# A decoder block's FFN: up-projection with stationary activations, down-projection by a scheme of seven block products

## The chip, the core and the metric

One of the cores of a Trainium2 chip runs the kernel. The metric is the time of one execution on the device in microseconds (us). The profile is of one execution, and its times are microseconds from the first instruction.

TensorE (PE in the profile) multiplies a stationary operand that was loaded into it (PEld) with a moving one and adds into banks of PSUM. VectorE (DVE), ScalarE (ACT) and GpSimd (POOL) work on elements, SyncE (SP) issues transfers.

## What is computed

One layer with 256 tokens of 2048 channels. `mix` comes from a gated convolution, a causal pooling and a cross-attention into 256 memory tokens; the change leaves that part as it was. D_FF is 5632.

```python
h = rmsnorm(x, g_mix)
...
x = x + mix @ w_out
h = rmsnorm(x, g_ffn)
u = causal_dwconv(h @ w_up, ffn_conv_w) + ffn_conv_b     # 3 taps, per channel
gate, val = jnp.split(u, 2, axis=-1)                     # 5632 channels each
x = x + (silu(gate) * val) @ w_down
return rmsnorm(x, g_final)
```

## The kernel before

**Split precision.** Every factor of a product is held as two parts: a high part, rounded to the type that TensorE multiplies at full rate, and a low part, the rest. A product is three matmuls: high by high, low by high, high by low.

**The stream of weights.** All weights pass in tiles of 1 MB. `next_tile` hands out the next one and runs ahead: `load` issues the transfer on SyncE's queue three tiles ahead (three `raw` buffers), and two tiles ahead `split_piece` has ScalarE copy the high part (L129) and VectorE subtract it for the low part (L130), into three buffers each.

**Up-projection.** `unit_a` and its `mm_a` hold the weights stationary: for each chunk of 128 inputs and 128 outputs the weights' high part multiplies the activations' high and low parts side by side (512 columns, L306), their low part the high parts (256 columns, L309). The result lies with channels in the partitions and tokens in the columns. A unit is 256 channels of gate and of value; there are 22. `up_finish` adds the two halves and multiplies by the row of the tokens' norms (`gather`, L322 to L324), and applies the convolution: one ScalarE operation for the last tap and the bias (L747), two of VectorE for the other taps (L751), and silu for the gate (L755). `up` multiplies gate and value (L776) and splits them into the tile `u` (L777, L778).

**Down-projection.** The units are done in groups of 8, 7, 5 and 2. `down` holds the activations stationary and streams 512 columns of weights (`mm_b`, L338, L341, L344) into eight banks, and `add_in` adds these into the residual `xt` (L706). A group's down-projection stands after the next group's first unit. `down_last` does the last group, four chunks of 128 channels, in pieces with the final norm between them.

**Order.** In the first and the last part the instructions of an engine keep the order of the program. Elsewhere a scheduler sets each engine's order before the run, and from then on every engine works in that order.

Of the kernel before, what the change touches and what calls it, by code (L numbers as in the profile page):

```python
# [24 lines left out]
def kernel(  # L25
# [23 lines left out]
    psum = ctx.enter_context(tc.tile_pool(name="psum", bufs=8, space=bass.MemoryType.PSUM))  # L49

    def bank(name):
        return psum.tile([P, 512], F32, tag="bank", name=name)

# [17 lines left out]
    # Per-channel vectors, as columns of 128 channels, by transposing rows of 128.  # L71
# [20 lines left out]
    rows = lambda v: v.rearrange("(r c) -> r c", c=P)  # noqa: E731  # L92
# [10 lines left out]
    stream = []  # (source, nk, ncol, pieces)  # L103
# [4 lines left out]
    def load(i, between=None):  # L108
        src, nk, ncol, pieces = stream[i]
        raw = wpool.tile([P, nk, ncol], F32, tag="raw", name=f"raw_{i}")  # L110
# [23 lines left out]
    def split_tile(i):  # L134
        nk, pieces = stream[i][1], stream[i][3]
        step = nk // pieces
        for j in range(0, nk, step):
            split_piece(i, j, j + step)
        loaded.pop(i)
# [16 lines left out]
    n_units = NF // 2  # L156
    UNITS = [8, 7, n_units - 17, 2]  # sizes of FFN groups in units of 256 channels
# [20 lines left out]
    # The pool's weights: per pair of groups the three chunks' rows, in the columns of  # L178
    # the output chunks that they reach; wp_at[k] is the first of them.
# [17 lines left out]
    # Chunks of the mix in the order in which they come about.  # L197
# [10 lines left out]
    # A group's down-projection comes after the next group's first unit; that of the  # L208
    # last but one after all units.
    sched = []  # L210
    done = 0
    for gi, (a, n) in enumerate(group_of):
        upto = n_units if gi + 2 >= len(group_of) else a + n + 1
        for u in range(done, upto):
            sched.append(("up", u, [g for g, (b, m) in enumerate(group_of) if b <= u][-1]))
        done = upto
        sched.append(("down", gi, None))
    for what, a, b in sched:
        if what == "up" and a == 0:
            for h in (0, 1):  # L220
                plan_a(w_up, 0, (h,))
                plan_a(w_up, D_UP, (h,))
        elif what == "up":
            plan_a(w_up, a * 256)
            plan_a(w_up, D_UP + a * 256)
        else:
            a0, n = group_of[a]
            for n2 in range(2):
                plan_b(w_down, a0 * 2, n * 2, n2 * 1024, 1024, 2)

# [1 line left out]
    def turn_pair(xt, k, nm):  # L232
        pt = bank(f"pt_{nm}_{k}")
# [24 lines left out]
    def rstd_of(ssq, nm):  # L258
        """ssq [P, n] sums of squares -> 1 / sqrt(mean + eps), with a Newton step."""
# [14 lines left out]
    def row_of(r, nm):  # L274
        """[P, TB] per-token values -> the same row of S values in every partition."""
# [44 lines left out]
    def gather(ps, row, o, engine=nc.vector):  # L320
        """(main + corrections) * row -> o [P, S] in SBUF."""
# [4 lines left out]
    def mm_b(ps, wt, actT, ks, tbs, first, last):  # L326
        """ps[tb][n] += act[tokens of tb, chunk k] @ w[chunk k, columns of n]."""
# [398 lines left out]
    def up_matmul(u):  # L726
        if u:
            return [unit_a(h2T, f"g{u}"), unit_a(h2T, f"v{u}")]
# [197 lines left out]
```

## Time and profile before

| | |
|---|---|
| time, median of 3 runs | 1065.43 us (1064.88 to 1066.43) |
| span of the profiled execution, first to last instruction | 1064.7 us |
| TensorE busy | 1054.7 us, 99% |
| VectorE busy | 703.6 us, 66% |
| ScalarE busy | 529.0 us, 50% |
| GpSimd busy | 43.1 us, 4% |
| moved by DMA | 202.01 MB, mean 190 GB/s |

The profiled execution's own time is its span; no other time of it is given. A row of a group gives line, engine, operation, output and input with their shapes and the count, then the busy time and the mean of one in nanoseconds, then the engine's idle time ahead of them and what ended it. In a timeline a row is start, duration and instruction; rows that follow each other closely overlap. In the chain the share of an engine is the part of the span in which the end waited for it.

### The profile page before, as it was taken

The numbers are of one execution on the slowest core, as the hardware profiler recorded it, in microseconds if no ns is written. First come the engines' busy times: TensorE is split into PE (matmuls) and PEld (weight loads), VectorE is DVE, ScalarE is ACT, GpSimd is POOL, SyncE is SP. The second block draws the span as 40 slices with busy tenths as digits, with TensorE's granted clock in tenths as the row PEclk, the third lists the DMA queues.
The fourth block names the chain that finished last, engine by engine and source line by source line (L and its number), as shares of the span: only waits on it lengthen the run. The fifth ranks groups of instructions, "written<-read, shape, count | busy, mean of one in ns | idle before, by whom it ended". The sixth has DMA issues, their size and how long they took to land.

```text
span 1064.7 us, 14249 instructions
## 1 busy us (share of the span) xinstructions
PE 1054.7 (99%) x5632; PEld 907.2 (85%) x5632; DVE 703.6 (66%) x920; ACT 529.0 (50%) x683; POOL 43.1 (4%) x163
## 2 busy tenths in 40 slices
PE   9999999999999999999999999999999999999996
PEld 8888898888888888888888888888888888888885
DVE  5677786764556777777744467777754477777655
ACT  5965454443446655555533344554533345555343
POOL 0023500000000000000000000000000000000000
PEclk9999999999999999999999999999999999999998
DMA  9765465455555556555555555655555555654552
GB/s 316 243 224 172 143 206 189 161 195 183 186 185 174 184 196 198 188 181 185 198 198 198 196 171 187 198 185 175 195 198 197 191 174 190 198 177 178 198 198 80
DMA packets 147342, 202.01 MB, mean 190 GB/s; under 512 B 3619, under 2 KB 125771, under 8 KB 147147
## 3 DMA queue, kind: packets, MB, share of 16 engines
q1 hardware_dynamic: 147242, 201.09, 55.8%
q8 instruction: 44, 0.72, 0.3%
q14 instruction: 24, 0.19, 0.0%
q10 hardware_dynamic: 32, 0.01, 0.0%
HBM read 198.99 MB, written 2.10 MB: 189 GB/s over the span
## 4 chain that ended last, share of the span: by engine, by line
PE 98%; DVE 1%; ACT 0%; issue 0%; DVEq 0%
PE pa_v L306 15%; PE pa_g L306 15%; PE pa_g L309 7%; PE pa_v L309 7%; PE pd L338 7%; PE pd L344 7%; PE pd L341 7%; PE po L338 3%; PE po L341 3%; PE po L344 3%; PE pa_cc L306 2%; PE pa_cx L306 2%; PE pa_cb L306 2%; PE pa_pv L306 2%; PE pk L395 2%; PE pa_q L306 1%
## 5 line engine op out<-in xcount | busy, mean ns | idle before, releaser
L130 DVE TENSOR_TENSOR lo<-raw,hi 128x2048 fp32r<-128x2048 f32 (+2 forms) x196 | 425.5, 2172 | 271.6 <-ACT hi L129 270.6
L129 ACT ACTIVATE hi<-raw 128x2048 fp32r<-128x2048 f32 (+2 forms) x196 | 355.9, 1818 | 255.8 <-PE pd L344 98.4
L306 PE MATMUL pa_v<-h2T,hi 128*128 128x512 f32 x672 | 236.7, 396 | 0.0
L306 PE MATMUL pa_g<-h2T,hi 128*128 128x512 f32 x672 | 236.7, 396 | 0.0
L309 PE MATMUL pa_g<-h2T,lo 128*128 128x256 f32 x672 | 188.5, 281 | 0.0
L309 PE MATMUL pa_v<-h2T,lo 128*128 128x256 f32 x672 | 188.5, 281 | 0.0
L306 PEld LDWEIGHTS pa_v<-h2T,hi 128*128 128x128 f32 x672 | 126.0, 188 | 30.0
L306 PEld LDWEIGHTS pa_g<-h2T,hi 128*128 128x128 f32 x672 | 126.0, 188 | 30.0
L309 PEld LDWEIGHTS pa_g<-h2T,lo 128*128 128x128 f32 x672 | 127.0, 189 | 0.1
L309 PEld LDWEIGHTS pa_v<-h2T,lo 128*128 128x128 f32 x672 | 127.0, 189 | 0.0
L338 PE MATMUL pd<-hi,u 128*128 128x512 f32 x320 | 98.6, 389 | 0.0
L341 PE MATMUL pd<-lo,u 128*128 128x512 f32 x320 | 98.5, 389 | 0.0
L344 PE MATMUL pd<-hi,u 128*128 128x512 f32 x320 | 98.5, 389 | 0.0
L751 DVE SCALAR_TENSOR_TENSOR t<-h,cols,t 128x256 f32<-128x256 f32 x176 | 79.1, 480 | 2.2 <-ACT t L747 1.4
L755 ACT ACTIVATE t<-t 128x256 f32<-128x256 f32 x44 | 18.3, 418 | 107.0 <-DVE t L751 107.0
L341 PEld LDWEIGHTS pd<-lo,u 128*128 128x128 f32 x320 | 60.1, 188 | 12.6
L344 PEld LDWEIGHTS pd<-hi,u 128*128 128x128 f32 x320 | 60.1, 188 | 12.4
L338 PEld LDWEIGHTS pd<-hi,u 128*128 128x128 f32 x320 | 59.9, 188 | 12.4
L747 ACT ACTIVATE t<-h,cols 128x256 f32<-128x256 f32 x88 | 49.8, 593 | 0.0
L322 ACT ACTIVATE h<-pa_g 128x256 f32<-128x256 f32 x42 | 16.0, 380 | 61.3 <-PE pa_g L309 61.3
L338 PE MATMUL po<-hi,mixT 128*128 128x512 f32 x128 | 39.6, 391 | 0.0
L341 PE MATMUL po<-lo,mixT 128*128 128x512 f32 x128 | 39.5, 389 | 0.0
(207 smaller groups left out, 1280.9 us busy)
## 6 DMA issues: line engine op xcount, KB each, us to landing
raw<-in_w_up_dram SPq DMA_DIRECT2D x88, 1024.0 KB, 5.0
raw<-in_w_down_dram SPq DMA_DIRECT2D x44, 1024.0 KB, 4.9
raw<-in_w_in_dram SPq DMA_DIRECT2D x28, 1024.0 KB, 4.9
raw<-in_w_out_dram SPq DMA_DIRECT2D x16, 1024.0 KB, 4.9
raw<-in_w_kv_dram SPq DMA_DIRECT2D x4, 1024.0 KB, 5.2
raw<-in_w_kv_dram SPq DMA_DIRECT2D x6, 512.0 KB, 8.3
memt<-in_mem_dram SPq DMA_DIRECT2D x8, 256.0 KB, 7.7
xt<-in_x_dram SPq DMA_DIRECT2D x4, 512.0 KB, 6.7
```

The source lines that it names most:

```text
L129: nc.scalar.activation(hi[:, s, :], raw[:, s, :], AF.Copy)
L130: nc.vector.tensor_tensor(lo[:, s, :], raw[:, s, :], hi[:, s, :].bitcast(F32), op=ALU.subtract)
L306: nc.tensor.matmul(ps[mi], hi[:, kk, c], actT[:, k, :], start=first and kk == 0, stop=False)
L309: nc.tensor.matmul(ps[mi][:, S:], lo[:, kk, c], actT[:, k, :S], start=False, stop=last and kk == nk - 1,)
L322: nc.scalar.activation(o, ps[:, S:], AF.Copy)
L338: nc.tensor.matmul(ps[tb][n], ah, hi[:, kk, c], start=f, stop=False)
L341: nc.tensor.matmul(ps[tb][n], ah, lo[:, kk, c], start=False, stop=False)
L344: nc.tensor.matmul(ps[tb][n], al, hi[:, kk, c], start=False, stop=l)
L395: nc.tensor.matmul(psk[mi], wt[0][:, j, c], mT[:, k, :], start=k == 0, stop=False)
L747: nc.scalar.activation(t, hp[:, 2:], AF.Identity, bias=cvec("ffn_conv_b", m), scale=cw[2])
L751: nc.vector.scalar_tensor_tensor(t, hp[:, s : s + S], cw[s], t, op0=ALU.mult, op1=ALU.add)
L755: nc.scalar.activation(t, t, AF.Silu)
```

## The change

**Up-projection.** A unit is 512 channels; there are 11, in groups of two and a last one alone. `up(u, b)` does one weight tile, four chunks of inputs by 512 channels: for each of the two blocks of 128 tokens the activations are stationary and the weights move, 24 matmuls of 512 columns. The eight tiles of a unit are four of the gate and four of the value. The result has tokens in the partitions, so the norm becomes a scale per partition in ScalarE's copy out of PSUM (L842), and `up_finish` turns it back by eight transposes (L853) into PSUM, from which ScalarE (L861) and VectorE (L863) do the convolution. This is put off through `todo` until the first half of the next up tile is issued.

**Down-projection.** But for the last unit, the 8 chunks of a group and 1024 columns of output make a block (two blocks a group, ten in all). With the activations cut into four blocks (two token blocks by even and odd chunks) and the weights into four (b11, b12, b21, b22), seven products of 12 matmuls each stand for eight. `turn` makes the sums of activation blocks in `sums`, with their high and low parts (L895 to L905). The sums of weight blocks are made in three buffers of 1 MB as the stream runs: b11+b12 and then b22 by VectorE (L247), b12+b22 and b11+b21 by an accumulating transfer from buffer to buffer that GpSimd issues (`add_far`, L244). After its sum, each is split as a tile of the stream (L254, L255). The block b21 is loaded into the buffer of b12, and so after the fourth product's split. `prod` adds the bank of a chain into `xt` after each product (L933).

**Order of the stream.** The list `after` says how many products of the group before follow each up tile: in a group of 16 up tiles none after the first three, one after each of the next twelve, two after the last; in the last group of eight tiles one after each of six, then two, then six. The scheduler moves some of it.

**Buffers.** The PSUM banks are opened again for the FFN, five for up tiles and transposes and three for the products. `sums` and `ffn` take the place of the tiles `u`; the last unit's activations go into a part of `h2T`.

```diff
-    UNITS = [8, 7, n_units - 17, 2]  # sizes of FFN groups in units of 256 channels
+    n_units = NF // 4
+    UNITS = [2] * (n_units // 2) + [1]
...
+    class Blocks:
+        def __init__(self, seq, gi, p):
+            self.seq, self.gi, self.p = seq, gi, p
+            self.k0 = group_of[gi][0] * 4
+        def buf(self, name):
+            at = {"b11": 0, "b22": 1, "b12": 2, "b21": 2}[name]
+            return rawd[(self.seq + at) % 3]
+        def load(self, name):
+            s, h = int(name[1]) - 1, int(name[2]) - 1
+            c0 = self.p * 1024 + h * 512
+            src = w_down[self.k0 * P : (self.k0 + 8) * P, c0 : c0 + 512]
+            src = src.rearrange("(j s p) c -> s p j c", s=2, p=P)[s]
+            nc.sync.dma_start(self.buf(name), src)
+        def add_far(self, to, what):
+            nc.gpsimd.dma_start(self.buf(to), self.buf(what), accum_op=ALU.add)
+        def add(self, to, what):
+            nc.vector.tensor_tensor(self.buf(to), self.buf(to), self.buf(what), op=ALU.add)
+        def split(self, i, idx):
+            raw = self.buf(("b11", "b11", "b11", "b12", "b22", "b21", "b11")[idx])
+            hi, lo = split[i] = [
+                wpool.tile([P, 4, 512], F32R, tag=t, name=f"{t}_{i}") for t in ("hi", "lo")
+            ]
+            nc.scalar.activation(hi, raw, AF.Copy)
+            nc.vector.tensor_tensor(lo, raw, hi.bitcast(F32), op=ALU.subtract)
+            if idx == 0:
+                self.add("b11", "b12")
+                self.add_far("b12", "b22")
+            elif idx == 1:
+                self.add("b11", "b22")
+            elif idx == 3:
+                self.load("b21")
+                self.add_far("b11", "b21")
+            elif self.next is not None and idx >= 4:
+                self.next.load({4: "b11", 5: "b22", 6: "b12"}[idx])
...
-    sched = []
+    for gi, (a, n) in enumerate(group_of):
+        n_t = 8 * n
+        if not prods:
+            after = [0] * n_t
+        elif n == 2:
+            after = [0, 0, 0] + [1] * 12 + [2]
+        else:
+            after = [1, 1, 1, 1, 1, 1, 2, 6]
+        assert sum(after) == len(prods)
+        for t in range(n_t):
+            sched.append(("up", a + t // 8, t % 8))
+            for _ in range(after[t]):
+                sched.append(prods.pop(0))
+        if gi < len(group_of) - 1:
+            prods = [("prod", b, i) for b in blocks[2 * gi : 2 * gi + 2] for i in range(N_PROD)]
+    for what, a, b in sched:
+        if what == "up":
+            w, q = part_of(a, b)
+            plan_b(w_up, 4 * q, 4, w * D_UP + a * 512, 512, 4)
+        elif what == "prod":
+            stream.append((a, None, b, 1))
+    a0, n = group_of[-1]
+    for n2 in range(2):
+        plan_b(w_down, a0 * 4, n * 4, n2 * 1024, 1024, 2)
...
-    row_2 = None
-    u_tiles = {}
-    def up_matmul(u):
-        if u:
-            return [unit_a(h2T, f"g{u}"), unit_a(h2T, f"v{u}")]
-        ps = [[bank(f"pu0_{w}_{mi}") for mi in range(2)] for w in range(2)]
-        for h in range(2):
-            for w in range(2):
-                mm_a(ps[w], next_tile(), h2T, h * 8, 8, h == 0, h == 1)
-                if h == 0 and w == 0:
-                    transpose_in(xt, h2T, "g_ffn", range(8, 16), "x2")
-        return ps
...
+    psum_ctx.close()
+    for kind, n in (("pool", 5), ("prod", 3)):
+        psum[kind] = ctx.enter_context(
+            tc.tile_pool(name=f"psum_{kind}", bufs=n, space=bass.MemoryType.PSUM)
+        )
+    sums = apool.tile([P, N_PROD + 1, 2, 4, P], F32R, tag="act", name="sums")
+    ffn = apool.tile([P, 4, 2048], F32, tag="act", name="ffn")
+    u_raw = ffn[:, 0, :].rearrange("p (c t) -> p c t", t=S)
+    rawd = [ffn[:, 1 + i, :].rearrange("p (j c) -> p j c", c=512) for i in range(3)]
+    for name in ("b11", "b22", "b12"):
+        blocks[0].load(name)
+    u_last = h2T[:, : 4 * UNITS[-1], :]
+    up_ps, up_gates, todo, r_2 = {}, {}, [], []
+    def up(u, b):
+        w, q = part_of(u, b)
+        if q == 0:
+            up_ps[w] = [bank(f"pu{u}_{w}_{tb}") for tb in range(TB)]
+        ps = up_ps[w]
+        hi, lo = next_tile()
+        for tb in range(TB):
+            for kk in range(4):
+                k = 4 * q + kk
+                ah = h2T[:, k, tb * P : (tb + 1) * P]
+                al = h2T[:, k, S + tb * P : S + (tb + 1) * P]
+                for n, (x_, y_) in enumerate(((ah, hi), (ah, lo), (al, hi))):
+                    nc.tensor.matmul(
+                        ps[tb], x_, y_[:, kk, :],
+                        start=k == 0 and n == 0, stop=k == KC - 1 and n == 2,
+                    )
+            if tb == 0 and todo:
+                todo.pop(0)()
+            r_2.append(rstd_sum(ssq4, "x2"))
+        if q < 3:
+            return
+        z = []
+        for tb in range(TB):
+            z.append(spool.tile([P, 512], F32, tag="w2k", name=f"z_{u}_{w}_{tb}"))
+            nc.scalar.activation(z[tb], ps[tb], AF.Copy, scale=r_2[0][:, tb : tb + 1])
+        todo.append(lambda: up_finish(u, w, z))
+    def up_finish(u, w, z):
+        pt = []
+        for c in range(4):
+            if c % 2 == 0:
+                pt.append(bank(f"pz{u}_{w}_{c}"))
+            for tb in range(TB):
+                o = c % 2 * S + tb * P
+                nc.tensor.transpose(pt[-1][:, o : o + P], z[tb][:, c * P : (c + 1) * P], ident)
+        outs = []
+        for c in range(4):
+            v = pt[c // 2][:, c % 2 * S : (c % 2 + 1) * S]
+            m = w * NF + u * 4 + c
+            tag, n, bufs = ("w1k", S, 6) if w else ("hpad", PAD + S, HPAD)
+            t = spool.tile([P, n], F32, tag=tag, name=f"t_{u}_{w}_{c}", bufs=bufs)[:, :S]
+            cw = [cvec("ffn_conv_w", j * 2 * NF + m) for j in range(3)]
+            nc.scalar.activation(t, v, AF.Identity, bias=cvec("ffn_conv_b", m), scale=cw[2])
+            for s in (1, 2):
+                nc.vector.scalar_tensor_tensor(
+                    t[:, s:], v[:, : S - s], cw[2 - s], t[:, s:], op0=ALU.mult, op1=ALU.add
+                )
+            if w == 0:
+                nc.scalar.activation(t, t, AF.Silu)
+            outs.append(t)
+        if w == 0:
+            up_gates[u] = outs
+            return
+        gates = up_gates.pop(u)
+        gi = [g for g, (a, n) in enumerate(group_of) if a <= u][-1]
+        for c in range(4):
+            if gi < len(group_of) - 1:
+                o = u_raw[:, (u - group_of[gi][0]) * 4 + c, :]
+                nc.vector.tensor_tensor(o, gates[c], outs[c], op=ALU.mult)
+            else:
+                nc.vector.tensor_tensor(gates[c], gates[c], outs[c], op=ALU.mult)
+                split_into(u_last[:, c, :], gates[c])
+        if gi < len(group_of) - 1 and u == group_of[gi][0] + group_of[gi][1] - 1:
+            turn(gi)
+    def turn(gi):
+        v = u_raw.rearrange("p (j s) (b t) -> p s b j t", s=2, b=TB)
+        a11, a12, a21, a22 = v[:, 0, 0], v[:, 1, 0], v[:, 0, 1], v[:, 1, 1]
+        t = wpool.tile([P, 4, 4, P], F32, tag="raw", name=f"turn_{gi}")
+        tt = nc.vector.tensor_tensor
+        parts = [(0, a11), (5, a12), (6, a22)]
+        for at, src in parts:
+            nc.scalar.activation(sums[:, at, 0], src, AF.Copy)
+        tt(t[:, 0], a21, a22, op=ALU.subtract)
+        tt(t[:, 2], a11, a21, op=ALU.subtract)
+        tt(t[:, 1], t[:, 0], a11, op=ALU.subtract)
+        for at, src in parts[:1]:
+            tt(sums[:, at, 1], src, sums[:, at, 0].bitcast(F32), op=ALU.subtract)
+        tt(t[:, 3], t[:, 1], a12, op=ALU.add)
+        nc.scalar.activation(sums[:, 1:5, 0], t, AF.Copy)
+        for at, src in parts[1:]:
+            tt(sums[:, at, 1], src, sums[:, at, 0].bitcast(F32), op=ALU.subtract)
+        tt(sums[:, 1:5, 1], t, sums[:, 1:5, 0].bitcast(F32), op=ALU.subtract)
+    chains = {}
+    def prod(bl, i):
+        hi, lo = next_tile()
+        chain, first, tb, right, op = (
+            ("a", True, 0, 0, ALU.add),
+            ("b", True, 1, 1, ALU.add),
+            ("a", False, 0, 1, ALU.subtract),
+            ("a", False, 1, 1, ALU.subtract),
+            ("b", False, 0, 1, ALU.add),
+            ("c", True, 0, 0, ALU.add),
+            ("a", False, 1, 0, ALU.add),
+        )[i]
+        if first:
+            chains[chain] = bank(f"pp_{bl.seq}_{chain}", "prod")
+        ps = chains[chain]
+        for j in range(4):
+            ah, al = sums[:, i, 0, j, :], sums[:, i, 1, j, :]
+            for n, (a, b) in enumerate(((ah, hi), (ah, lo), (al, hi))):
+                nc.tensor.matmul(
+                    ps, a, b[:, j, :], start=first and j == 0 and n == 0,
+                    stop=j == 3 and n == 2, skip_group_check=True,
+                )
+        c0 = bl.p * 1024 + right * 512
+        o = xt[:, tb, c0 : c0 + 512]
+        nc.vector.tensor_tensor(o, o, ps, op=op)
+        while todo and bl.gi == len(blocks) // 2 - 1 and i == 2:
+            todo.pop(0)()
...
```

**Where the instructions stand.** The first place is the start of the last group, on VectorE. Before, a unit's end on VectorE looked like this (`lo` is a weight tile's low part, `t` and `h` the unit's channels, `u` the activations for the down-projection, `pa` PSUM):

```order
L776 TENSOR_TENSOR t_0_1_7106<-t_0_1_7106,t_1_1_7203 128x256
L130 TENSOR_TENSOR lo_7256<-raw_7215,hi_7255 128x2048
L778 TENSOR_TENSOR u_6376<-t_0_0_7096,u_6376 128x256
L778 TENSOR_TENSOR u_6376<-t_0_1_7106,u_6376 128x256
L323 TENSOR_TENSOR h_0_0_7291<-pa_g_0_7213,h_0_0_7291 128x256
L324 TENSOR_TENSOR h_0_0_7291<-h_0_0_7291,row_x_3031 128x256
L130 TENSOR_TENSOR lo_7316<-raw_7253,hi_7315 128x2048
```

Now, after the last unit of the last whole group, the sums of activations follow (`turn` is their scratch tile, `ffn` at L247 two weight blocks):

```order
L877 TENSOR_TENSOR ffn<-t_0_3_6861,t_1_3_7107 128x256
L900 TENSOR_TENSOR sums<-ffn,sums 128x512
L896 TENSOR_TENSOR turn_7115<-ffn 128x512
L904 TENSOR_TENSOR sums<-ffn,sums 128x512
L898 TENSOR_TENSOR turn_7115<-turn_7115,ffn 128x512
L904 TENSOR_TENSOR sums<-ffn,sums 128x512
L901 TENSOR_TENSOR turn_7115<-turn_7115,ffn 128x512
L247 TENSOR_TENSOR ffn<-ffn 128x2048
L905 TENSOR_TENSOR sums<-turn_7115,sums 128x4x512
L933 TENSOR_TENSOR xt<-xt,pp_a 128x512
L136 TENSOR_TENSOR lo_7162<-raw_7140,hi_7161 128x2048
```

The first product needs the low sum of L900, the next one that of L905; between them stand five smaller operations and one sum of weight blocks.

On TensorE the first product of that group stands behind the second up tile, one tile later than the list says (`hi_7069` is that tile's high part, `hi_7048` the first product's):

```order
L827 MATMUL pu_0_1_7068<-hi_7069,h2T 128x512
L927 MATMUL pp_a<-hi_7048,sums 128x512 [waits Activation_49]
L927 MATMUL pp_a<-lo_7049,sums 128x512
L927 MATMUL pp_a<-hi_7048,sums 128x512 [waits DVE_49]
L927 MATMUL pp_a<-hi_7048,sums 128x512
```

The third of these is the first that uses a low part of the activations' sums, and waits for VectorE, which makes it.

The second place is ScalarE at the seventh product of a block. Before, in a down-projection stretch, the high parts followed each other:

```order
L777 ACTIVATE u_7813<-t_0_1_8107 128x256
L129 ACTIVATE hi_8280<-raw_8248 128x2048
L129 ACTIVATE hi_8310<-raw_8278 128x2048
L129 ACTIVATE hi_8340<-raw_8308 128x2048
L129 ACTIVATE hi_8378<-raw_8338 128x2048
```

Now (with the semaphores waited for; DMASW is a transfer that GpSimd issued, `z` the copies of an up tile out of PSUM):

```order
L254 ACTIVATE hi_6975<-ffn 128x2048 [waits DMAHW7_49,DVE_49,PE_49]
L254 ACTIVATE hi_6995<-ffn 128x2048 [waits DMASW7_49,DVE_49,PE_49]
L842 ACTIVATE z_1_0_7024<-pu_1_0_6818,r_x_2908 128x512 [waits PE_49]
L842 ACTIVATE z_1_1_7026<-pu_1_1_6819,r_x_2908 128x512 [waits PE_49]
L135 ACTIVATE hi_7028<-raw_6993 128x2048 [waits DMAHW6_49,DVE_49]
```

Behind the high part that waits for the accumulating transfer (`hi_6995`) stand the copies of the up tile and the next tile's high part.

More of the change, by code (lines that the diff above doesn't have):

```diff
@@ L48, with bank @@
     spool = ctx.enter_context(tc.tile_pool(name="spool", bufs=2))
-    psum = ctx.enter_context(tc.tile_pool(name="psum", bufs=8, space=bass.MemoryType.PSUM))
-    def bank(name):
-        return psum.tile([P, 512], F32, tag="bank", name=name)
+    psum_ctx = ExitStack()
+    psum = {"pool": psum_ctx.enter_context(tc.tile_pool(name="psum", bufs=8, space=bass.MemoryType.PSUM))}
+    def bank(name, kind="bank"):
+        if "prod" not in psum:
+            return psum["pool"].tile([P, 512], F32, tag="bank", name=name)
+        return psum["prod" if kind == "prod" else "pool"].tile([P, 512], F32, tag=kind, name=name)
     ident = cpool.tile([P, P], F32, name="ident")
@@ L135, in split_tile @@
         nk, pieces = stream[i][1], stream[i][3]
+        if nk is None:
+            stream[i][0].split(i, stream[i][2])
+            return
         step = nk // pieces
@@ L153, in next_tile @@
         return split.pop(i)
-    n_units = NF // 2
-    UNITS = [8, 7, n_units - 17, 2]
+    n_units = NF // 4
+    UNITS = [2] * (n_units // 2) + [1]
+    assert sum(UNITS) == n_units and NF % 4 == 0
     D_UP = DFF
@@ L210, with part_of @@
+    blocks = []
+    for gi in range(len(group_of) - 1):
+        for p in range(2):
+            blocks.append(Blocks(len(blocks), gi, p))
+            if len(blocks) > 1:
+                blocks[-2].next = blocks[-1]
+    def part_of(u, b):
+        return (b // 2 % 2, b % 2 + b // 4 * 2) if u == 0 else (b // 4, b % 4)
     sched = []
-    done = 0
+    prods = []
     for gi, (a, n) in enumerate(group_of):
[L213 to L217, printed above, removed]
@@ L218 @@
-    for what, a, b in sched:
[L219 to L233, printed above, removed]
+        n_t = 8 * n
@@ L737, in up_finish @@
-    def up_finish(ps, u, w):
-        outs = []
-        for mi in range(2):
-            m = w * NF + u * 2 + mi
-            hp = spool.tile([P, S + 2], F32, tag="hpad", name=f"h_{u}_{w}_{mi}", bufs=HPAD)
-            nc.gpsimd.memset(hp[:, :2], 0.0)
-            gather(ps[mi], row_2, hp[:, 2:])
-            t = spool.tile([P, S], F32, tag="w1k", name=f"t_{u}_{w}_{mi}", bufs=6)
+    psum_ctx.close()
[3 more added lines that the diff above has]
+        )
@@ new lines @@
+    sums = apool.tile([P, N_PROD + 1, 2, 4, P], F32R, tag="act", name="sums")
[24 more added lines that the diff above has]
+                todo.pop(0)()
+        if u == 0 and b == 0:
+            for k in range(8, 16, 2):
+                split_turned(turn_pair(xt, k, "x2", "prod"), h2T, "g_ffn", k)
+            r_2.append(rstd_sum(ssq4, "x2"))
+        if q < 3:
+            return
+        z = []
[3 more added lines that the diff above has]
+        todo.append(lambda: up_finish(u, w, z))
@@ L782, in down @@
-    def down(gi):
-        ut = u_tiles[gi]
-        nk = group_of[gi][1] * 2
-        for n2 in range(2):
-            ps = [[bank(f"pd_{gi}_{n2}_{tb}_{n}") for n in range(2)] for tb in range(TB)]
-            for i in range(nk // 2):
-                mm_b(ps, next_tile(), ut, (2 * i, 2 * i + 1), range(TB), i == 0, i == nk // 2 - 1)
-            add_in(ps, n2 * 2, range(TB), f"d{gi}")
+        if w == 0:
+            up_gates[u] = outs
+            return
+        gates = up_gates.pop(u)
+        gi = [g for g, (a, n) in enumerate(group_of) if a <= u][-1]
@@ L888 @@
     for what, a, b in sched:
-        if what == "up":
-            up(a, b)
-        elif a < len(group_of) - 1:
-            down(a)
-        else:
-            down_last(a)
+        (up if what == "up" else prod)(a, b)
+    down_last(len(group_of) - 1)
 _INS = [
```

39 lines of the change are left out of this document (8 added, 31 removed).

## The prediction

> **What bounds the kernel now.** I read the page's busy shares first, then the chain that ended last, then the granted clock.
>
> ```profile
> span 1064.7 us, 14249 instructions
> PE 1054.7 (99%) x5632; PEld 907.2 (85%) x5632; DVE 703.6 (66%) x920; ACT 529.0 (50%) x683; POOL 43.1 (4%) x163
> ...
> PEclk9999999999999999999999999999999999999998
> ...
> PE 98%; DVE 1%; ACT 0%; issue 0%; DVEq 0%
> ```
>
> TensorE is busy 99% of the span at full clock and carries 98% of the chain. So a matmul less is time less, at its rate in the stream, as long as the other engines keep its operands ready. They have room on average (VectorE 66%, ScalarE 50%); the windows show it by stage, first an up-projection stretch, then a down-projection stretch (columns: busy time of PE, PEld, DVE, ACT, POOL, clock, DMA share, GB/s):
>
> ```profile
> 475.00:500.00 25.00, 25.00 (x146) 22.05 (x146) 19.37 (x27) 12.04 (x17) 0.40 (x4) 1.00 0.53 174
> 518.00:543.00 25.00, 25.00 (x118) 20.88 (x117) 16.70 (x19) 11.44 (x13) 0.30 (x3) 1.00 0.54 196
> ```
>
> Next the groups by shape, which give the price of each operation, and two rows of the waits:
>
> ```profile
> L130 DVE TENSOR_TENSOR lo<-raw,hi 128x2048 fp32r<-128x2048 f32 x175 | 401.4, 2294 | 264.8 <-ACT hi L129 264.5
> L129 ACT ACTIVATE hi<-raw 128x2048 fp32r<-128x2048 f32 x175 | 335.2, 1915 | 255.8 <-PE pd L344 98.4 <-issue 84.2 <-PE po L344 39.2
> L751 DVE SCALAR_TENSOR_TENSOR t<-h,cols,t 128x256 f32<-128x256 f32 x176 | 79.1, 480 | 2.2 <-ACT t L747 1.4
> L747 ACT ACTIVATE t<-h,cols 128x256 f32<-128x256 f32 x88 | 49.8, 593 | 0.0
> L776 DVE TENSOR_TENSOR t<-t,t 128x256 f32<-128x256 f32 x44 | 16.8, 420 | 0.0
> L755 ACT ACTIVATE t<-t 128x256 f32<-128x256 f32 x44 | 18.3, 418 | 107.0 <-DVE t L751 107.0
> L706 DVE TENSOR_TENSOR xt<-pd,xt 128x512 f32<-128x512 f32 x24 | 14.9, 683 | 0.0
> L709 ACT ACTIVATE jk_o<-xt 128x512 f32<-128x512 f32 x8 | 5.0, 622 | 5.9 <-DVE xt L706 5.9
> ```
>
> ```profile
> DVE lo L130 <- ACT hi L129: 270.6, 168, 3.2
> ...
> ACT hi L129 <- PE pd L344: 98.4, 28, 3.5
> ```
>
> A weight tile costs 1.92 us on ScalarE and then 2.29 on VectorE, and the split waits for TensorE to free a buffer: the weights run ahead of TensorE, not behind it.
>
> **The change, part by part.** The rate of the stream, from TensorE's timeline: the first and the last row of a down-projection stretch (19 rows, 36 matmuls of 512 columns from the first start to the last), and of an up-projection stretch (11 pairs of 512 and 256 columns). The rows' own durations overlap, so I take starts.
>
> ```profile
> 525.77 0.61 PE L344 MATMUL pd<-hi,u 128*128 128x512 f32 x2
> ...
> 533.93 0.39 PE L344 MATMUL pd<-hi,u 128*128 128x512 f32 x1
> ```
>
> ```profile
> 618.00 0.40 PE L306 MATMUL pa_g<-h2T,hi 128*128 128x512 f32 x1
> ...
> 621.89 0.40 PE L306 MATMUL pa_v<-h2T,hi 128*128 128x512 f32 x1
> ```
>
> That is 8.16/36 = 0.2267 us for 512 columns and 3.89/11 = 0.3536 for a pair.
>
> Up-projection: 22 units x 2 halves x 16 chunks x 2 = 1408 pairs, 497.9 us, become 11 units x 2 x 16 chunks x 2 token blocks x 3 = 2112 matmuls of 512, 478.8. That gives **-19.1**. A weight load per matmul is hidden as in the down-projection now, whose form it takes.
>
> Down-projection: 40 chunks x 2 x 4 x 3 = 960 matmuls become 10 blocks x 7 products x 12 = 840: 120 x 0.2267 = **-27.2**. The last group's share is unchanged.
>
> Transposes back: 22 groups of 8, between matmuls, as here:
>
> ```profile
> 297.66 1.04 PE L237 MATMUL pt_x<-ident,xt 128*128 128x128 f32 x8
> 298.46 0.70 PE L338 MATMUL po<-hi,mixT 128*128 128x512 f32 x2
> 299.00 0.63 PE L341 MATMUL po<-lo,mixT 128*128 128x512 f32 x2
> ```
>
> Eight take 0.80, and the next pair starts 0.54 later instead of 0.45: 0.89 x 22 = **+19.6**. The small product for the row of norms goes (under 0.3, left out). TensorE alone thus gives 1064.7 - 26.7 = 1038.0. What remains is what it has to wait for.
>
> Start of the FFN: the banks are opened anew, so the first up tile waits for the last addition of the output projection, with which it now overlaps:
>
> ```profile
> 319.26 2.48 DVE L706 TENSOR_TENSOR xt<-po,xt 128x512 f32<-128x512 f32 x4
> ...
> 320.34 0.39 PE L306 MATMUL pu<-h2T,hi 128*128 128x512 f32 x1
> ```
>
> 319.26 + 2.48 = 321.74 against 320.34; the additions can start a little earlier, so **+1**.
>
> A steady group (16 up tiles, 14 products) is 16 x 5.44 + 14 x 2.72 + 4 x 0.89 = 128.7 us of TensorE. VectorE in it: 30 low parts x 2.29, 4 sums of weight blocks at the same size 9.2, the sums of the activations 7 x 0.68 + 2.29 = 7.1, 32 x 0.48 of convolution, 8 x 0.42 of products, 14 x 0.68 into xt: 113 us, 88%. ScalarE: 30 x 1.92, 8 copies out of PSUM and 3 for the sums at 0.62, one at 1.92, 16 x 0.59, 8 x 0.42: 79 us, 61%. Both fit on average. The tight place is the head: the first product comes after four up tiles (22.7 us), and the sums it needs are there after about 19 (worked out for the last group below, plus two more low parts); the second product's at 30 against 30.8. I allow 0.5 a group, **+2** for four.
>
> The two sums by DMA: they take 4 of 8 block sums off VectorE, and GpSimd and its queue have nothing else here (4% busy, nearly all early). An accumulating DMA is not in this trace; call its time A. The nearest rows are the loads of 1 MB, and the window with the highest traffic:
>
> ```profile
> raw<-in_w_up_dram SPq DMA_DIRECT2D x88, 1024.0 KB, 5.0
> raw<-in_w_down_dram SPq DMA_DIRECT2D x44, 1024.0 KB, 4.9
> ```
>
> ```profile
> 354.00:360.00 6.00, 6.00 (x37) 5.30 (x36) 5.32 (x8) 3.81 (x6) 0.00 (x0) 1.00 0.98 328
> ```
>
> Lower end: as a load, 4.9. Upper: it reads two blocks and writes one while loads share the engines; 3 MB at 328 GB/s is 9.6, and with as much again from loads beside it 19. A load moves each byte twice (read, write) and this one three times, so 4.9 x 1.5 = 7.4; I take 8. The Trainium skill's page "DMA: Bandwidth & Descriptors", section "Anatomy of one DMA — SWDGE (gpsimd) path", gives a copy of this kind 2.0 us and its bytes at 436 GB/s, 4.4 for 1 MB, with no price for accumulating; by that the sum below would come out some 3.6 us lower, and no run here shows it yet. In a steady group A is hidden up to a bound. The low part of the fourth product is done 4 to 6 us after the third starts; then b21 is loaded (5.0), then A, then high and low part of the seventh (4.2), which is due 2.7 + 3 x 5.44 + 3 x 2.72 = 27.2 after the third's start: A may be 12 to 14, I take 12.5. Up to there the cost is nothing; beyond, each us costs one in each of four groups, since ScalarE is in order and holds the next tiles' high parts behind that wait.
>
> The last group is short: 8 up tiles for 14 products, and no tile between the last five. Its head, from the first up tile's start: VectorE adds into xt (0.7), sums blocks (2.3), makes a low part (2.3), then 8 x 0.48, 4 x 0.42, a low part, a difference and the first low sum (1.4): 14.2 or about 14. The product is due after two tiles and the transposes, 11.8: 2.2 late. Then 5 x 0.68 + 2.3 + 2.3 = 8.0 to the other sums, at 22.0, where the second product needs them at 17.4: 4.6 late, and the next tile 0.5. Together 7.3.
>
> Its tail, from the start T of the first block's seventh product (P6; the second block's are Q0 to Q6). The load of b12 starts when P6's low part is done, T-4, and lands at T+1; VectorE's sum ends at T+3.3, the first accumulation at T+11.3. Q3's low part is ready at T+17.8, TensorE is there at 18.1 (it lost 1.1 at Q2, behind VectorE). b21 loads into the freed buffer until 22.9, the second accumulation ends at 31, high and low part of Q6 at 35.2; Q6 then ends at 37.5. Without waits it would end at T + 8 x 2.72 + 5.44 + 0.89 = 28.1: 9.4 late. Head and tail: **+17**.
>
> Sum: 1038.0 + 1 + 2 + 17 = 1058.0 of span; the runs' median lies 0.7 above the span, so **1059**.
>
> **Rivals.** *Hidden after all* (chance 0.16). Convolution rows follow each other faster than their mean, and A may be near 4.9 (the tail's 9.4 becomes 6.3); if the head's stall halves as well, 5 to 10 us go: **1047**. Against it: VectorE's queue in the head is a sum of single rows.
>
> *The accumulation is slow* (0.20), the one that ends on the other side. At A = 16 the tail grows by 8 for the second accumulation and 6 for the first (it had 2 to spare), each steady group by 3.5: 28 more, **1087**. It decides from A = 12.5 on, where the tail's 7 alone reaches the old time. For it: the upper bound reaches 19, and loads are at 0.53 DMA share already. Against: the share leaves half the engines' time.
>
> *VectorE falls behind in steady groups* (0.12). At 88% in order, a low part behind a convolution that waits for its transposes stops TensorE for about one low part and one sum more each group: 4 x 3, and as little again: 12 to 14, **1072**. Before, the up stretch ran at 19.37 of 25 (77%) without a gap.
>
> *The clock falls in the last group's gaps* (0.08). The end of the trace shows it; TensorE's last matmul is in the first window here:
>
> ```profile
> 1050.00:1056.00 6.00, 5.98 (x40) 5.29 (x38) 4.52 (x13) 1.96 (x7) 0.00 (x0) 1.00 0.15 58
> 1056.00:1058.00 2.00, 0.00 (x0) 0.00 (x0) 1.66 (x7) 0.72 (x3) 0.00 (x0) 1.00 0.58 222
> 1058.00:1060.00 2.00, 0.00 (x0) 0.00 (x0) 1.93 (x5) 0.00 (x0) 0.00 (x0) 0.63 0.50 187
> 1060.00:1062.00 2.00, 0.00 (x0) 0.00 (x0) 1.04 (x2) 0.00 (x0) 0.00 (x0) 0.50 0.82 312
> ```
>
> The granted clock goes to 0.50 about 2.5 us after TensorE stops. Three of my gaps are as long; a product after each at half clock costs 2.7 more, 8 in all: **1067**. The Trainium skill's page "TensorE: Matmul & The Clock Gate", section "Why this matters for your kernels", wants no idle gap over about 3 us, since one idle window halves the clock; by that rule all three gaps count and this rival's time follows, and the rows above agree with it.
>
> **How the numbers follow.** This kernel's measurement tells 0.2% (2.1 us) from no change, so faster is under 1063.3 and slower over 1067.6. My forecast has 0.44, with its own range 1052 to 1066: 0.36 faster, 0.08 same. Hidden: 0.16 faster. Slow accumulation: 0.20 slower. VectorE behind: 0.02 faster, 0.10 slower. Clock: 0.04 same, 0.02 faster, 0.02 slower. Sums: 0.56 faster, 0.12 same, 0.32 slower. For 8 in 10 the range takes in the first rival but for its fast end, and the slow accumulation up to A = 16: 1044 to 1088.
>
> **What would show it.** TensorE's busy time near 1028, its stream at 0.2267 in both projections and 0.89 for eight transposes; its idle time in the last 110 us, in the head on the sums and in the tail on high and low parts of Q2, Q5 and Q6; ScalarE's high part of the seventh product waiting on GpSimd's queue there only. Wrong it would be if such waits stood in every group, if the accumulations landed later than 12 us, if the clock row showed dips, or if the matmul rate of the up-projection were not that of the down-projection.

## The result and the profile after

The changed kernel takes 1068.51 us (median of 5 runs, 1067.35 to 1069.71) against 1065.19 beside it: ratio 1.0033, 95% interval 1.0021 to 1.0046. It is slower by 0.3%, where a gain of 0.6% was forecast. The profiled run took 1067.88 us, its span is 1066.1.

The page after, its shares, slices, clock and chain:

```profile
span 1066.1 us, 12610 instructions
PE 1040.6 (98%) x4982; PEld 868.6 (81%) x4982; DVE 794.2 (74%) x840; ACT 591.7 (56%) x648; POOL 51.6 (5%) x95
...
PE   9999999999999999999999999999999999989976
...
PEclk9999999999999999999999999999999999989988
...
PE 91%; DVE 4%; DMA 2%; ACT 2%; issue 1%; DVEq 0%; ACTq 0%; POOLq 0%
```

TensorE has 14 us less of busy time than before, and the span is longer: it now waits, and the chain has 9% of other engines. The two rows of slices say where: only in the last five of forty, with the clock down there too (the last slice is as low before, since TensorE ends ahead of the kernel). The windows tell the stages apart, the four steady groups first, then three places in the last group:

```profile
415.66:544.70 129.04, 129.04 (x588) 107.15 (x587) 107.36 (x97) 76.16 (x67) 3.62 (x4) 1.00 0.75 228
544.70:673.50 128.80, 128.80 (x584) 106.69 (x583) 106.75 (x97) 75.75 (x66) 3.42 (x4) 1.00 0.75 228
673.50:802.50 129.00, 128.99 (x585) 106.88 (x585) 107.05 (x97) 75.84 (x67) 3.44 (x4) 1.00 0.75 228
802.50:931.50 129.00, 129.00 (x586) 106.85 (x585) 106.99 (x97) 75.81 (x67) 3.44 (x4) 1.00 0.73 220
942.00:955.00 13.00, 9.94 (x28) 7.07 (x29) 13.00 (x14) 7.08 (x7) 0.00 (x0) 0.74 0.32 110
944.00:947.00 3.00, 3.00 (x8) 2.34 (x8) 3.00 (x6) 0.54 (x2) 0.00 (x0) 0.56 0.00 0
1020.00:1036.00 16.00, 11.70 (x36) 8.10 (x35) 12.63 (x16) 8.60 (x9) 0.86 (x1) 0.79 0.36 79
```

A steady group takes 129.0 us with TensorE never idle, at full clock, and VectorE at 83%. What is lost to waits is lost in the last group. From the end of its first transposes (931.36) to the first matmul of the third product (954.71) TensorE has 62 matmuls, 14.1 us at 0.2267, and takes 23.3: 9.3 lost in the head. From there to its last matmul (1057.2) it has 88.6 us of work and takes 102.5: 13.9 lost in the tail. Together 23.2, of which the rows with idle time ahead of them hold 13.4. Of the other 9.8 some 6 are matmuls at about half the granted clock (one each 0.43 us), about 1.5 in each of four stretches: 943.7 to 947.0, 950.4 to 953.6, 1025.1 to 1028.6 and 1031.9 to 1035.3. The rest lies at the ends and the starts of the stream around the gaps.

TensorE's first matmul of the last group's up tiles and its rows with idle time in the head, then two of VectorE's rows there (the sums that the first and the second product wait for):

```profile
927.84 0.39 PE L827 MATMUL pu<-hi,h2T 128*128 128x512 f32 x1
...
935.27 0.50 PE L827 MATMUL pu<-lo,h2T 128*128 128x512 f32 x1 [0.45 <-DVE lo L136]
...
942.42 0.50 PE L927 MATMUL pp_a<-hi,sums 128*128 128x512 f32 x1 [1.86 <-ACT sums L895]
...
943.69 1.22 PE L927 MATMUL pp_a<-hi,sums 128*128 128x512 f32 x2 [0.53 <-DVE sums L900]
...
948.65 0.50 PE L927 MATMUL pp_b<-hi,sums 128*128 128x512 f32 x1 [1.04 <-ACT sums L902]
...
950.45 1.22 PE L827 MATMUL pu<-hi,h2T 128*128 128x512 f32 x2 [1.06 <-ACT hi L135]
```

```profile
942.95 0.69 DVE L900 TENSOR_TENSOR sums<-ffn,sums 128x512 fp32r<-128x512 f32 x1
...
948.76 2.29 DVE L905 TENSOR_TENSOR sums<-turn,sums 128x2048 fp32r<-128x2048 f32 x1
```

And in the tail, TensorE first, then VectorE, then SyncE's queue (the loads of b12 and b21 of the last block), then GpSimd (the last accumulation) and ScalarE, which waits for it:

```profile
1000.70 0.50 PE L827 MATMUL pu<-lo,h2T 128*128 128x512 f32 x1 [1.60 <-DVE lo L136]
...
1011.16 0.50 PE L927 MATMUL pp_a<-lo,sums 128*128 128x512 f32 x1 [0.95 <-DVE lo L255]
...
1016.16 0.50 PE L927 MATMUL pp_b<-lo,sums 128*128 128x512 f32 x1 [1.64 <-DVE lo L255]
...
1023.88 0.50 PE L927 MATMUL pp_c<-lo,sums 128*128 128x512 f32 x1 [1.83 <-DVE lo L255]
...
1029.04 0.50 PE L927 MATMUL pp_a<-hi,sums 128*128 128x512 f32 x1 [1.17 <-ACT hi L254]
1030.84 0.73 PE L413 MATMUL pl<-hi,h2T 128*128 128x512 f32 x2 [1.30 <-ACT hi L135]
```

```profile
996.15 2.29 DVE L247 TENSOR_TENSOR ffn<-ffn 128x2048 f32<-128x2048 f32 x1 [3.80 <-DMA ffn<-in_w_down_dram]
998.36 2.29 DVE L136 TENSOR_TENSOR lo<-raw,hi 128x2048 fp32r<-128x2048 f32 x1
...
1008.81 4.49 DVE L255 TENSOR_TENSOR lo<-ffn,hi 128x2048 fp32r<-128x2048 f32 x2 [2.57 <-ACT hi L254]
...
1029.02 2.29 DVE L255 TENSOR_TENSOR lo<-ffn,hi 128x2048 fp32r<-128x2048 f32 x1 [2.82 <-ACT hi L254]
```

```profile
989.58 0.37 SPq L241 DMA_DIRECT2D ffn<-in_w_down_dram  x1
...
1013.34 0.37 SPq L241 DMA_DIRECT2D ffn<-in_w_down_dram  x1
```

```profile
1020.03 0.86 POOL L244 DMA_DIRECT2D ffn<-ffn  x1 [20.43 <-DVE t L863]
```

```profile
1027.08 1.91 ACT L254 ACTIVATE hi<-ffn 128x2048 fp32r<-128x2048 f32 x1 [4.53 <-DMA ffn<-ffn]
```

VectorE stands 3.80 us idle at a sum of weight blocks whose b12 is still on its way (6.6 us from the issue of that load to the sum's start), and the last up tile's low part, which needs nothing of it, is queued behind. Later b21 is loaded into the buffer that the fourth product's split has just left (6.1 us), then accumulated (7 us), then split, and TensorE has only the fifth and the sixth product to do between.

### The profile page after: what moved, and what is told of

Read it like the earlier page. It is cut to its first block, busy times and chain, and to the rows that moved or that the text cites. A ratio compares the mean times of both kernels' runs of the same rounds, so it can differ in the third digit from the quotient of the medians.

```text
span 1066.1 us, 12610 instructions
## 1 busy us (share of the span) xinstructions
PE 1040.6 (98%) x4982; PEld 868.6 (81%) x4982; DVE 794.2 (74%) x840; ACT 591.7 (56%) x648; POOL 51.6 (5%) x95
## 4 chain that ended last, share of the span: by engine, by line
PE 91%; DVE 4%; DMA 2%; ACT 2%; issue 1%; DVEq 0%; ACTq 0%; POOLq 0%
PE pu L827 44%; PE pp_a L927 9%; PE pp_b L927 5%; PE po L419 3%; PE po L416 3%; PE po L413 3%; PE pa_cx L381 2%; PE pa_cc L381 2%; PE pa_cb L381 2%; PE pa_pv L381 2%; PE pp_c L927 2%; PE pz L853 2%; PE pk L470 1%; PE pa_q L381 1%; DMA ffn<-in_w_down_dram 1%; PE pa_cb L384 1%
## 5 line engine op out<-in xcount | busy, mean ns | idle before, releaser
L827 PE MATMUL pu<-hi,h2T 128*128 128x512 f32 x1408 | 450.0, 391 | 2.4 <-DVE xt L781 1.4
L136 DVE TENSOR_TENSOR lo<-raw,hi 128x2048 fp32r<-128x2048 f32 (+3 forms) x156 | 333.3, 2138 | 122.3 <-ACT hi L135 121.3
L135 ACT ACTIVATE hi<-raw 128x2048 fp32r<-128x2048 f32 (+3 forms) x156 | 279.3, 1793 | 123.9 <-PE po L419 39.3
L827 PEld LDWEIGHTS pu<-hi,h2T 128*128 128x128 f32 x1408 | 264.4, 188 | 57.5 <-issue 1.8
L827 PE MATMUL pu<-lo,h2T 128*128 128x512 f32 x704 | 274.5, 390 | 2.1 <-DVE lo L136 2.1
L255 DVE TENSOR_TENSOR lo<-ffn,hi 128x2048 fp32r<-128x2048 f32 x70 | 160.3, 2291 | 85.5 <-ACT hi L254 85.5
L254 ACT ACTIVATE hi<-ffn 128x2048 fp32r<-128x2048 f32 x70 | 133.8, 1915 | 112.0 <-PE pu L827 75.0
L827 PEld LDWEIGHTS pu<-lo,h2T 128*128 128x128 f32 x704 | 132.2, 188 | 30.2 <-DVE lo L136 3.6
L927 PE MATMUL pp_a<-hi,sums 128*128 128x512 f32 x320 | 107.5, 398 | 3.6 <-ACT sums L895 1.9
L863 DVE SCALAR_TENSOR_TENSOR t<-pz,cols,t 128x255 f32<-128x255 f32 (+1 forms) x176 | 79.6, 478 | 11.0 <-ACT t L861 10.0
L861 ACT ACTIVATE t<-pz,cols 128x256 f32<-128x256 f32 x88 | 46.9, 558 | 50.3 <-DVE t L863 26.9
L842 ACT ACTIVATE z<-pu,r_x 128x512 f32<-128x512 f32 x44 | 30.0, 685 | 43.8 <-PE pu L827 43.8
L244 POOL DMA_DIRECT2D ffn<-ffn x20 | 17.4, 868 | 678.2 <-DVE ffn L247 391.4
L247 DVE TENSOR_TENSOR ffn<-ffn 128x2048 f32<-128x2048 f32 x20 | 45.7, 2286 | 3.8 <-DMA ffn<-in_w_down_dram 3.8
```

Source lines behind the costliest of these rows:

```text
L135: nc.scalar.activation(hi[:, s, :], raw[:, s, :], AF.Copy)
L136: nc.vector.tensor_tensor(lo[:, s, :], raw[:, s, :], hi[:, s, :].bitcast(F32), op=ALU.subtract)
L254: nc.scalar.activation(hi, raw, AF.Copy)
L255: nc.vector.tensor_tensor(lo, raw, hi.bitcast(F32), op=ALU.subtract)
L827: nc.tensor.matmul(ps[tb], x_, y_[:, kk, :], start=k == 0 and n == 0, stop=k == KC - 1 and n == 2,)
L861: nc.scalar.activation(t, v, AF.Identity, bias=cvec("ffn_conv_b", m), scale=cw[2])
```

## The experiments

The theory (A): all the loss lies in the last group, in the waits of its head and tail and in the clock that falls behind them. The rival (B): the change costs in every group, through transposes, additions into `xt` and transfers, and the last group only shows it. The changed kernel was timed beside 1065.19 of the kernel before, the experiments beside 1064.7, so a difference between an experiment and the changed kernel is uncertain by about half a microsecond more than the intervals say.

**e1: no sums of activations in the last group**, whose products use those of the group before.

```diff
-        if gi < len(group_of) - 1 and u == group_of[gi][0] + group_of[gi][1] - 1:
+        if gi < len(group_of) - 2 and u == group_of[gi][0] + group_of[gi][1] - 1:
```

> Left out: the sums of activation blocks for the last group (its products use those of the group before). Theory A (the loss sits in the last group: about 14 us in which TensorE is idle and about 10 more in which it runs at half clock after the gaps): the head's gaps and its half clock go, about 9 us, so 1059 to 1061. Theory B (the loss is spread over all groups, through transposes, additions into xt and DMA traffic): within 2 us of the changed kernel's 1068.5. If VectorE's convolution and block sum, not the sums of activations, hold the head: 1064 to 1067.

1061.38 us, 7.1 less than the changed kernel (0.9973 of before, 0.9962 to 0.9984), where A expected about 9; it lies 0.4 above the upper end of A's range. In the head two short waits are left, on weights:

```profile
947.53 0.51 PE L927 MATMUL pp_a<-hi,sums 128*128 128x512 f32 x1 [0.69 <-ACT hi L254]
948.63 0.50 PE L827 MATMUL pu<-lo,h2T 128*128 128x512 f32 x1 [0.60 <-DVE lo L136]
```

The sums and their place in VectorE's queue hold the head; the tail kept its waits. B would have left it within 2 us. Whether a later place of the products alone, with the sums kept, would free the head was not tried.

**e2: no accumulating transfers in the last block.**

```diff
     def add_far(self, to, what):
+        if self.next is None:
+            return
```

> Left out: the two accumulating transfers of the last block of weights alone. Theory A with the second accumulation on the tail's chain (b21 loaded, accumulated, split): 5 to 9 us less than the changed kernel, 1060 to 1064, and the wait of the seventh product's high part on that transfer gone. If the first accumulation is on the path too, up to 12 less. Theory B: within 2 us of 1068.5.

1064.99 us, 3.5 less; A expected 5 to 9. The seventh product no longer waits for the transfer, but TensorE's rows still show waits of 0.3 to 1.7 us on low parts all through the tail. The accumulations are a quarter of the tail's loss, not most of it.

**e4: matmuls on no one's data in the gaps.**

```diff
+        n_fill = {(8, 0): 8, (8, 1): 8, (9, 4): 6, (9, 5): 8, (9, 6): 8}.get((bl.seq, i), 0)
+        if n_fill:
+            fill = bank(f"fill_{bl.seq}_{i}")
+            for _ in range(n_fill):
+                nc.tensor.matmul(fill, h2T[:, 15, :P], h2T[:, 15, :], start=True, stop=True)
```

> Added: 38 matmuls of 512 columns on no one's data (8.6 us at the stream's rate) around the first two products of the last group and the last three of its second block, where TensorE was idle; nothing left out. If the gaps cause the half clock and that costs about 10 us: the granted clock stays near 1.0 and the time falls by 3 to 8 us, to 1060 to 1065. If the slow matmuls have another cause, or the gaps only move: 1068 to 1075, since the added matmuls then cost time.

1069.21 us, no gain. The clock stayed up in the first product, and the next wait grew in its place; behind that wait and behind the last one of the tail it fell all the same (windows, the last one in the tail, then a row of TensorE):

```profile
940.00:944.00 4.00, 4.00 (x19) 3.15 (x18) 4.00 (x10) 2.10 (x4) 0.00 (x0) 1.00 0.72 269
944.00:948.00 4.00, 2.29 (x10) 1.52 (x9) 4.00 (x6) 1.55 (x2) 0.00 (x0) 1.00 0.01 2
948.00:952.00 4.00, 2.25 (x7) 1.32 (x8) 4.00 (x4) 4.00 (x3) 0.00 (x0) 0.94 0.00 0
952.00:956.00 4.00, 4.00 (x13) 3.18 (x12) 4.00 (x2) 0.86 (x2) 0.00 (x0) 0.63 0.93 312
1032.00:1036.00 4.00, 3.06 (x8) 2.35 (x9) 4.00 (x4) 3.00 (x3) 0.00 (x0) 0.68 0.00 0
```

```profile
948.68 0.50 PE L932 MATMUL pp_b<-hi,sums 128*128 128x512 f32 x1 [2.39 <-ACT sums L902]
```

The first product now runs at full clock and ends early, but the second starts at 948.68 instead of 948.65, since VectorE and ScalarE set that time. So the slow matmuls there filled a wait. Of the four stretches at half clock two stand ahead of a further wait, and two, some 3 us, behind the last wait of the head and of the tail. Those two e4 did not take away, and in the tail some of its matmuls outlasted their gap: the sixth product's low part is now waited for 0.15 us instead of 1.83, but its matmul starts 2.1 us later, 0.7 of them from ahead of the tail. So e4 does not price the clock behind a last wait. The expected fall of 3 to 8 us did not come.

**e5: plain products in the last group.** Its two blocks are done as eight products, each weight block split once and used for both token blocks, and the first product stands after the third up tile.

```diff
-            after = [1, 1, 1, 1, 1, 1, 2, 6]
+            after = [0, 0, 1, 1, 1, 1, 1, 3]
...
+            if gi >= n_seven:
+                prods = [("plain", (gi, p), q) for p in range(2) for q in range(4)]
...
+        if gi >= n_seven:       # in turn(): the four blocks themselves, no sums
+            for s in range(2):
+                for b in range(TB):
+                    nc.scalar.activation(sums[:, 2 * s + b, 0], v[:, s, b], AF.Copy)
+                    ...
```

> Changed: the last group's two blocks as plain products (8 instead of 7 a block, each of the four weight blocks split once and used for both token blocks; no sums of activations, no sums of weights), two up tiles later. Theory A: TensorE gets 4 products more... 2 products more (5.4 us) and loses the 24 us of waits and half clock: 1068.5 - 23.8 + 5.4 = 1050, clock 1.00 in the last group. Theory B: 1068.5 + 5.4 = 1074 less what the four additions give, 1072 to 1075.

1050.53 us, 0.9867 of before (0.9851 to 0.9884): 18.0 less than the changed kernel, with two products more, where A expected 1050. It changes three things at once: the eight products, no sums, and the later start; e1 and e10 take parts of it. No row of TensorE in the last group has an idle time ahead of it (its last matmul ends at 1040.0); the window and the clock's row:

```profile
931.00:1042.00 111.00, 109.04 (x515) 91.28 (x513) 72.45 (x91) 55.26 (x70) 0.00 (x0) 1.00 0.52 174
```

```profile
PEclk9999999999999999999999999999999999999998
```

**e10: only the last block plain**, the head as it was. The last block's four weight blocks enter the stream as ordinary tiles.

```diff
-            after = [1, 1, 1, 1, 1, 1, 2, 6]
+            after = [1, 1, 1, 1, 1, 1, 2, 3]
...
+                prods = prods[:N_PROD] + [("plain", (gi, 1), q) for q in range(4)]
```

> Changed: the changed kernel with only the last block's products plain (four split weight blocks, no sums of them); the head of the last group as it was. Of the 23.8 us lost in the last group 9.3 lie before the third product and 14.5 behind it by the trace. If these are separate: 1068.5 - 14.5 + 2.7 for one product more = 1057, with the head's waits still there. If the tail's loss is only pushed there by the head: under 1052. If the tail waits on VectorE's rate rather than on the chain of loads and sums: over 1061.

1058.21 us (0.9937, 0.9922 to 0.9952), 10.3 less, where 11.5 was expected. The head waits for the same sums as in the changed kernel, and no wait is left behind it:

```profile
942.83 0.50 PE L938 MATMUL pp_a<-hi,sums 128*128 128x512 f32 x1 [1.84 <-ACT sums L903]
...
949.05 0.50 PE L938 MATMUL pp_b<-hi,sums 128*128 128x512 f32 x1 [2.39 <-ACT sums L910]
950.85 1.22 PE L835 MATMUL pu<-hi,h2T 128*128 128x512 f32 x2 [1.07 <-ACT hi L135]
```

Head and tail are separate losses; the plain block takes away the whole chain of load, sum, load, accumulation. The first two rows also bear e4 out without added matmuls: from the first product's start to the second's are 6.22 us here, with a wait of 2.39 us, and 6.23 in the changed kernel, with a wait of 1.04 behind matmuls at half clock.

**e6: plain products in all groups**, the up-projection's part of the change alone: e5's code with no group by seven products.

```diff
-    N_PLAIN = 1
+    N_PLAIN = 5
...
-            after = [0, 0, 0] + [1] * 12 + [2]
+            after = [0, 0, 0] + [1, 0] * 5 + [1, 1, 1]
```

> Changed: all five groups with plain products as the last group in e5, so the up-projection's part of the change stands alone on an interleaved down-projection. If each product left out by the scheme is worth its 12 matmuls and nothing else (8 blocks with 7 for 8, 8 x 2.72 = 21.8 us): 1050.5 + 21.8 = 1072, and the up-projection part alone costs about 7 us against the kernel before. If the scheme's extra work on VectorE and DMA costs something in steady groups: under 1069. If plain groups wait themselves: over 1075.

1070.96 us (1.0061, 1.0044 to 1.0078). Behind the first up matmul no row of TensorE has a wait. The new up-projection, with the new groups and their order, costs 6.2 us by itself; its matmuls and transposes alone make 6.0 of it by the sums in the next section. The scheme in four steady groups is then worth 1070.96 - 1050.53 = 20.4, against 21.8 for its matmuls alone: nearly nothing is lost around it.

**e8: all four sums of weight blocks by VectorE**, in e5.

```diff
-                self.add_far("b12", "b22")
+            elif idx == 2:
+                self.add("b12", "b22")
...
-                self.add_far("b11", "b21")
+            if idx == 5:
+                self.add("b11", "b21")
```

> Changed: e5 with all four sums of weight blocks by VectorE, no accumulating transfer. VectorE gets 4 x 2.29 more in each of four steady groups, 116 of 129 us. If the transfers were only hidden work and VectorE has the room: 1050 to 1052. If VectorE in order has no room for them: 1054 to 1070, with TensorE idle on low parts in every group; then the two transfers are needed.

1050.17 us (0.9864, 0.9849 to 0.9879), the same as e5. VectorE's time in a steady stretch goes from 108.0 to 116.4 of 130 and TensorE still never waits (e8's window; the last two numbers are the DMA share and GB/s, 0.74 and 226 in e5):

```profile
545.00:675.00 130.00, 130.00 (x590) 107.66 (x589) 116.35 (x102) 75.93 (x66) 0.00 (x0) 1.00 0.59 194
```

So in the steady groups it makes no measurable difference whether VectorE or the transfers make these two sums.

**e7 and e7b: the old up-projection in e5.** Weights stationary again, no transposes; VectorE gets back the additions and the products with the norms.

```diff
-        for tb in range(TB):
-            ...                            # 24 matmuls of 512 columns
+        mm_a(up_ps[w], next_tile(), h2T, h * 8, 8, h == 0, h == 1)
...
+            gather(ps[mi], r_2[0], hp[:, 2:])
```

> Changed: e5 with the up-projection of the kernel before (weights stationary, 512 and 256 columns, no transposes back). TensorE's share of it was 494 us against 479 + 21 now, 6 us less: 1044 to 1046 if VectorE keeps up. VectorE gets the additions and the products with the row of norms instead, about 13.5 us more in each steady group: 120 of 127.5 us. If that stops TensorE: 1050 to 1065, idle TensorE on low parts in every group, and the transposed form then pays for itself through VectorE.

1077.71 us. Here the last two products of a group took the sums of the next one and waited for them, so part of the time came from where e7 put the sums of activations:

> Changed: as e7, but the sums of activations of a group stand behind the last two products of the group before in the program. In e7 they stood ahead of them, so that these two products took the next group's sums (a part of the computation that e7 changes) and waited for them. If that order made e7's stalls (5.8 us idle a group at its turn): 1050 or less. If VectorE's 113 us a group in order make them: 1060 to 1078, idle TensorE in the steady groups remains, and the transposed up-projection pays for itself through VectorE.

1065.30 us (0.9997, 0.9985 to 1.0008): 14.8 more than e5. The order had cost 12, yet the waits in the steady groups stay. Those shown come 13 and 23 us after VectorE's sums of activations, which end at 558.9:

```profile
572.00 0.50 PE L923 MATMUL pp_b<-hi,sums 128*128 128x512 f32 x1 [1.20 <-ACT hi L254]
582.22 0.51 PE L923 MATMUL pp_a<-hi,sums 128*128 128x512 f32 x1 [1.57 <-ACT hi L254]
583.00 0.60 PE L395 MATMUL pu<-h2T,lo 128*128 128x256 f32 x2 [0.27 <-DVE lo L136]
```

From 448.26 to 582.22, the same row of two groups, is 134.0 us, against 129.0 with the transposed form. VectorE's share of a stretch is 112 to 116 of 130, no more than in e8, where TensorE does not wait: its rate alone does not make the waits. That its queue's order does is likely but not shown, and which of its instructions is in the way was not tried. So the new up-projection loses 6 us by itself and is worth 15 beside the scheme, in these orders of the queues.

## Why the prediction was wrong

Faster was forecast, and it is slower. Point by point:

- **Up-projection, -19.1: mis-sized.** The sample of 11 pairs was taken at 618 us. Over whole half units of 32 pairs the kernel before shows two rates, by the first rows of a gate's and of its value's half in the second unit and in the ninth: 11.09 us in the first eight units, 11.29 to 11.31 in the later ones.

```profile
344.61 0.39 PE L306 MATMUL pa_g<-h2T,hi 128*128 128x512 f32 x1
...
355.70 0.39 PE L306 MATMUL pa_v<-h2T,hi 128*128 128x512 f32 x1
...
609.18 0.39 PE L306 MATMUL pa_g<-h2T,hi 128*128 128x512 f32 x1
...
620.47 0.40 PE L306 MATMUL pa_v<-h2T,hi 128*128 128x512 f32 x1
```

So all pairs are 494 us, not 498: -15.3. Why the first units run faster stays open.
- **Transposes, +19.6:** a group of 129.0 us less 552 matmuls at 0.2267 leaves 3.9 for four sets of eight, 0.97 each and +21.3 if all of it is theirs. The matmul just behind them takes 0.31 us (931.36 to 931.67 in the trace), and the ten after it 0.231 each there. Together with the up-projection +6.0, as e6 measured.
- **Down-projection, -27.2:** right as matmuls; e6 and e5 show 20.4 of 21.8 for the eight blocks of the steady groups.
- **Start, +1:** there was a wait of 1.4 us, but the first up matmul began at 320.02 instead of 320.34:

```profile
320.02 0.47 PE L827 MATMUL pu<-hi,h2T 128*128 128x512 f32 x1 [1.38 <-DVE xt L781]
```

- **Steady groups, +2:** no wait at all, and VectorE at 107 us, not 113.
- **Accumulation, 8 us, hidden in steady groups:** right. The 20 transfers took 6.9 to 10.2 us, 8.7 in the median:

```profile
DMA to landing us min/median/max: 6.9/8.7/10.2
```

The rival of a slow accumulation needed 12.5. By the Trainium skill's page "DMA: Bandwidth & Descriptors", section "Anatomy of one DMA — SWDGE (gpsimd) path", 4.4 us would be the estimate for a copy; the measured time is twice that, which the rule's price for copies does not cover.
- **Last group, +17: the step that failed.** The place and the kind of the waits were right, the size was not: it cost 23.2, the head 9.3 for 7.3, the tail 13.9 for 9.4.
  In the head the last sums of activations were there 23.2 us after the first up tile's start (927.84 to 951.05), for 22.0 in the working, and the matmuls behind that wait ran at half clock, 1.5 us more.
  The tail's working had b12 land at T+1, with P6's start at T. P6 began at 993.27, the load was issued at 989.58 and VectorE's sum of it started at 996.15, T+2.9; and the working left out that the last up tile's low part stands behind that sum in VectorE's queue (1.6 us of TensorE). So the low part of Q3 came at T+20.0 for T+17.8. From there b21's load took 6.1 instead of 5.0, and the low part of Q6 came at T+38.0 for T+35.2. Q6 itself, at half clock and with two matmuls of the last unit between its own, ended at T+42.3 for T+37.5.
- **The balance.** The first two lines and the last group make 3.8 + 1.7 + 6.2 us more, of which the steady groups and the start give 3.3 back: 8.4. The span was forecast at 1058.0 and is 1066.1, off by 8.1. The rest of the 9.5 us is the step from span to median: the runs' median lies 2.4 above the profiled span here, where the forecast took 0.7 from the kernel before. A run's time lies 1.7 to 2.0 above its own span wherever both are on record, so the profiled run before was by this the longest of its three. TensorE's busy time, forecast near 1028, is 1040.6: 5.5 by the first two lines and about 6 by the half clock.
- **The clock as a rival:** the dips came, as the rows show, and the time came out near that rival's 1067 by chance: its price, 2.7 us behind each of three gaps, is not what was measured. Two of the four stretches at half clock only filled a wait (e4 and e10 show it for the first), and the two behind a last wait hold about 3 us in all. The Trainium skill's page "TensorE: Matmul & The Clock Gate", section "Why this matters for your kernels", names gaps over about 3 us; here the clock was at 0.56 from 944 to 947 with no gap over 1.9 us ahead of it, several of them close together.

By experiments the balance is: up-projection +6.2 (e6 against before), scheme in the steady groups -20.4 (e6 to e5), last group by seven products +18.0 (e5 to the changed kernel). The three add up to +3.8 because each starts where the one before ends; side by side the two kernels differ by 3.3.

## What to carry to other kernels

A scheme that saves products by sums needs other work to hide the sums under; where the stream ends there is none, and 2 x 2.7 us saved there cost 23. Do the last group plainly, and count the queue of every engine through that group by hand, with what stands behind each wait. Slow matmuls ahead of a wait must not be added to it: see first which event ends the wait.

## What was not expected of the hardware

The granted clock fell to 0.56 after gaps of 0.5 to 1.9 us, none as long as the 2.5 us after which it fell at the end of the kernel before. A pair of matmuls with stationary weights took 0.3466 us in one stage and 0.3533 in another of the same kernel. The first matmul behind eight transposes took 0.31 us instead of 0.227. Twenty accumulations of 1 MB between buffers took 6.9 to 10.2 us beside a VectorE that was busy 83% of a steady group.
